# Two plain gate and up pairs become block products: eleven pairs by seven products each

## The chip, the cores and the metric

One core of a Trainium2 chip. The metric is device time in microseconds of one launch; a comparison is made between medians of runs of the kernel before and after. Engines: TensorE (PE, with PEld for its weight loads), VectorE (DVE), ScalarE (ACT), GpSimd (POOL) and SyncE (SP), which issues most loads.

## The reference

A decoder trunk with two layers on 512 positions of width 1024, all in float32. Layer 0 is a gated short convolution, layer 1 an attention layer over a window of 128 with shared keys and values; a SwiGLU feed-forward of width 2816 ends each layer.

```python
def swiglu(h, w_gate_up, w_down):
    g, u = jnp.split(h @ w_gate_up, 2, axis=-1)
    return (jax.nn.silu(g) * u) @ w_down
...
    for l in range(DEPTH):
        if l < N_A:
            mix = short_conv_mixer(rmsnorm(h, a_pre_norm[l]), a_w_in[l], a_conv_w[l], a_w_out[l])
            h = h + rmsnorm(mix, a_post_norm[l])
        else:
            ...
            attn = sliding_window_sink_attention(q, k_sh, v_sh, b_sinks[j]) @ b_w_o[j]
            h = h + rmsnorm(attn, b_post_norm[j])
        ff = swiglu(rmsnorm(h, ffn_pre_norm[l]), ffn_w_gate_up[l], ffn_w_down[l])
        h = h + rmsnorm(ff, ffn_post_norm[l])
```

## The kernel before, in words

Each matmul of the reference is three passes (`mm3`, L189 to L192): every float32 matrix is split into a high part and a low part (`whi`, `wlo` of a weight, `xhi`, `xlo` of an input), and low by high, high by high and high by low are added in PSUM. ACT makes a high part by a copy, DVE the low part by a subtraction. A weight is loaded by SP as a `raw` tile of 128 x 1024.

The gate and up weights come in 22 tiles of 128 columns each, f = 0 to 21, so eleven pairs of tiles. Pairs 0 and 1 (f below `PLAIN` = 4) are multiplied plainly. Pair 0 runs in `project_first`, into four PSUM banks (gate and up of f = 0 and 1), first for the positions 0 to 255 (half 0), then for 256 to 511 (half 1), while the last tile of the residual is still being turned into x. Pair 1 runs in `gate_plain`, 512 positions at a time. The other nine pairs use a scheme of seven products for a two by two block product (Strassen's form): the blocks are the halves of the positions by the halves of the 1024 inputs, and a product is 24 matmuls of 256 columns (two halves e of the gate and up columns, four blocks k, three passes). The order is P1, P2, P6, P5, P7, P3, P4; three accumulations X, Y and Z hold them, each in two banks, one for each e (`gate_jobs`, L850 to L915). P1, P2 and P3 take blocks of x as they are; P6, P5, P7 and P4 take sums of blocks of x, the factors, which `factors` (L356 to L378) makes on DVE with ACT's high parts, in parallel to pair 1. The sums of weight blocks are made by POOL's DMAs, which accumulate in HBM into `hsum` tiles (class `Sums`, L492; P5, P7, P6 and P3 use them); for a pair listed in `ADDED` only two of the four sums are made so, and DVE adds the other two (L445). The table `BEGIN` says at which place of the program a pair's sums are begun: "c" places are in the convolution, "o" in its projection, "a" in the attention, `0f1` or `0p2` in a feed-forward.

`Update` makes x: `take` and `scale` collect the projection, `mean`, `update` and `norm` apply two root mean squares, whose reciprocal root `ur` POOL computes; `turn` transposes four tiles into banks `xt`, `split` makes x hi on ACT (L336) and x lo on DVE (L337), and `keep` copies the parts of the sums (L354). `in_line` walks a list of jobs: each job's weight is fetched `N_RAW` ahead, and split three jobs (`LINE_LEAD`) ahead. Inside the feed-forward the order of instructions of every engine is the order of the program (`manual_schedule`); in the convolution and the projection a scheduler sets it. One launch runs, in time: convolution to about 139 us, its projection to 184, feed-forward 0 to about 510, keys, values and attention to about 690, projection and feed-forward 1 to the end.

Of the kernel before, what the change touches and what calls it, by code (L numbers as in the profile page):

```python
# [24 lines left out]
PLAIN = 4  # L25

ADDED = (0, 1, 2, 6, 7, 8)

BEGIN = {
# [4 lines left out]
}  # L34

ADDED = (0, 1, 2, 6, 7, 8)

BEGIN = {
# [23 lines left out]
NB = 4  # L62
# [12 lines left out]
def yoco_kernel(  # L75
# [10 lines left out]
    w_gu: bass.AP,  # L86
# [143 lines left out]
    class Update:  # L230
# [3 lines left out]
        def __init__(self, mix, gain, gpres, add):  # L234
            self.mix, self.gpres, self.add = mix, gpres, add
            self.gain = gain
# [93 lines left out]
        def split(self, n, f, hf):  # L330
            if self.x[n][f] is None:
                self.x[n][f] = (slot("xhi", F32R), slot("xlo", F32R))
            hi, lo = self.x[n][f]
            c = slice(hf * 256, (hf + 1) * 256)
            src = self.banks[f % 4, hf][:, (f // 4) * 256 : (f // 4 + 1) * 256]
            nc.scalar.activation(hi[:, c], src, AF.Copy, scale=g(self.gpres[n], f))  # L336
            nc.vector.scalar_tensor_tensor(  # L337
                out=lo[:, c], in0=src, scalar=g(self.gpres[n], f), in1=hi[:, c].bitcast(F32),
                op0=ALU.mult, op1=ALU.subtract,
            )  # L340

        def keep(self, b, hf, vector=False):

            for i in range(2):
                if (i, hf, b // 2) not in self.parts:
                    self.parts[i, hf, b // 2] = slot("part")
                out = self.parts[i, hf, b // 2][:, (b % 2) * 256 : (b % 2 + 1) * 256]
                src = self.banks[b, hf][:, i * 256 : (i + 1) * 256]
                gain = g(self.gpres[0], b + 4 * i)
                if vector:  # L350
                    nc.vector.tensor_scalar(out=out, in0=src, scalar1=gain, scalar2=None,
                                            op0=ALU.mult)
                else:
                    nc.scalar.activation(out, src, AF.Copy, scale=gain)  # L354

        def factors(self):  # L356


            x = self.x[0]
            made = {p: [] for p in range(1, 8)}  # L360
            for p, k0, c in ((1, 0, 0), (2, 4, 0), (3, 4, 256)):
                made[p] = [[a[:, c : c + 256] for a in x[k0 + k]] for k in range(4)]
            for j in range(2):
                q11, q21, q12, q22 = (self.parts[i, hf, j] for hf in range(2) for i in range(2))

                nc.vector.tensor_tensor(out=q11, in0=q11, in1=q12, op=ALU.subtract)
                nc.vector.tensor_tensor(out=q12, in0=q22, in1=q12, op=ALU.subtract)
                nc.vector.scalar_tensor_tensor(out=q22, in0=q22, scalar=-1.0, in1=q11,
# [63 lines left out]
    class Job:  # L432
# [14 lines left out]
        def prepare(self):  # L447
            if not self.raws:
                return
# [9 lines left out]
    def in_line(jobs, late):  # L459
# [21 lines left out]
        for j, job in enumerate(jobs):  # L481
# [5 lines left out]
            if late and not job.alone:  # L487
                late.pop(0)()
# [197 lines left out]
    def tile_done(res, t, ahead=None, square=True):  # L686
# [8 lines left out]
        if t > 0:  # L695
            res.norm(t - 1)
# [830 lines left out]
```

## Time and profile before

| | us |
|---|---|
| median of three runs | 1044.12 (1041.91 to 1044.95) |
| span of the profiled execution | 1043.2 |
| TensorE busy in it | 1031.6 (99%) |
| DVE busy | 761.4 (73%) |
| ACT busy | 552.5 (53%) |
| POOL busy | 170.6 (16%) |

The span runs from the first to the last instruction. A busy time counts an instruction from start to end, and matmuls overlap. In a row of the timeline stand start, length, engine, line, operation, what is written from what, and in brackets the idle time before it and what released it.

### The profile page before, as it was taken

Reading aid. Unit: us, or ns where it says so; the run is one execution under the profiler, and the core shown is the slowest. Engines: PE = TensorE matmul, PEld = TensorE weight load, DVE = VectorE, ACT = ScalarE, POOL = GpSimd, SP = SyncE. Lnnn points to the kernel's source line nnn. Section 1 sums busy time; section 2 is a strip of 40 time slices with the busy share of each in tenths; the row PEclk is TensorE's granted clock in tenths of the full one; section 3 lists DMA queues with packets and bytes.
Section 4 is the critical chain, followed back from the end, with each engine's and each line's share of the span. In section 5 each row is a group of like instructions: output and inputs, shape, how many; then the busy total and the mean of one; then the engine's idle time right before and its main releaser. Section 6 shows DMA issues by size and latency. Waiting matters only on the chain.

```text
span 1043.2 us, 17017 instructions
## 1 busy us (share of the span) xinstructions
PE 1031.6 (99%) x6556; PEld 931.4 (89%) x6556; DVE 761.4 (73%) x1280; ACT 552.5 (53%) x994; POOL 170.6 (16%) x227
## 2 busy tenths in 40 slices
PE   9999999999999999999999999999999999999997
PEld 7888888989879899999898888889998999989986
DVE  5675645488676978776658998685886777896754
ACT  7222235746645455464466777666565554645531
POOL 0322231122201000000021554211211110000001
PEclk9999999999999999999999999999999999999999
DMA  9657798568969955337413588967789697534521
GB/s 333 229 176 242 183 321 303 135 184 266 316 232 311 348 175 195 123 120 233 172 42 98 145 250 234 311 215 223 177 283 339 197 322 246 184 125 159 173 89 80
DMA packets 61297, 221.48 MB, mean 212 GB/s; under 512 B 7200, under 2 KB 8096, under 8 KB 51488
## 3 DMA queue, kind: packets, MB, share of 16 engines
q1 hardware_dynamic: 48608, 140.04, 37.2%
q0 software_dynamic: 12032, 79.70, 29.7%
q8 instruction: 51, 0.84, 0.3%
q10 hardware_dynamic: 576, 0.66, 0.2%
q14 instruction: 30, 0.25, 0.1%
HBM read 214.08 MB, written 85.98 MB: 288 GB/s over the span
## 4 chain that ended last, share of the span: by engine, by line
PE 89%; DVE 4%; DMA 3%; issue 1%; ACT 1%; POOLq 0%; POOL 0%; DVEq 0%; SPq 0%; ACTq 0%
PE gx L192 6%; PE gx L191 6%; PE gx L190 6%; PE pmix L191 5%; PE pmix L192 5%; PE pmix L190 5%; PE gz L192 3%; PE gz L191 3%; PE gz L190 3%; PE pgu L190 3%; PE pgu L191 3%; PE pgu L192 3%; PE px L190 2%; PE px L191 2%; PE px L192 2%; PE pcub L594 2%
## 5 line engine op out<-in xcount | busy, mean ns | idle before, releaser
L455 DVE TENSOR_TENSOR wlo<-raw,whi 128x1024 fp32r<-128x1024 f32 (+1 forms) x188 | 227.7, 1214 | 94.4 <-ACT whi L454 94.4
L454 ACT ACTIVATE whi<-raw 128x1024 fp32r<-128x1024 f32 (+1 forms) x188 | 194.6, 1049 | 82.7 <-DVE raw L445 26.6
L190 PE MATMUL gx<-xt,whi 128*128 128x256 f32 x432 | 122.3, 283 | 0.0
L191 PE MATMUL gx<-xt,whi 128*128 128x256 f32 x432 | 122.3, 283 | 0.0
L192 PE MATMUL gx<-xt,wlo 128*128 128x256 f32 x432 | 122.3, 283 | 0.0
L190 PEld LDWEIGHTS gx<-xt,whi 128*128 128x128 f32 x432 | 82.9, 192 | 0.0
L191 PEld LDWEIGHTS gx<-xt,whi 128*128 128x128 f32 x432 | 82.9, 192 | 0.0
L192 PEld LDWEIGHTS gx<-xt,wlo 128*128 128x128 f32 x432 | 82.9, 192 | 0.0
L521 POOL DMA_DIRECT2D hsum<-in_w_gb_dram x84 | 55.9, 717 | 120.5 <-ACT whi L454 81.0
L872 ACT ACTIVATE st<-gx 128x256 f32<-128x256 f32 x72 | 27.5, 381 | 84.2 <-PE gx L192 84.2
L289 POOL TENSOR_TENSOR ur<-uv,mhalf 128x1 f32<-128x1 f32 x15 | 11.6, 774 | 358.3 <-DVE uv L285 358.3
L185 ACT ACTIVATE whi<-raw 128x1024 fp32r<-128x1024 f32 x30 | 31.8, 1058 | 65.3 <-PE pb L191 26.3
L190 PE MATMUL pgu<-xlo,whi 128*128 128x256 f32 (+1 forms) x192 | 61.6, 321 | 0.0
L191 PE MATMUL pgu<-xhi,whi 128*128 128x256 f32 (+1 forms) x192 | 61.1, 318 | 0.0
L192 PE MATMUL pgu<-xhi,wlo 128*128 128x256 f32 (+1 forms) x192 | 61.1, 318 | 0.0
L186 DVE TENSOR_TENSOR wlo<-raw,whi 128x1024 fp32r<-128x1024 f32 x30 | 49.7, 1665 | 2.9 <-ACT whi L185 2.9
L190 PE MATMUL pmix<-wlo,ahi 128*128 128x512 f32 (+1 forms) x136 | 51.3, 377 | 0.0
L191 PE MATMUL pmix<-whi,ahi 128*128 128x512 f32 (+1 forms) x136 | 51.2, 377 | 0.0
L192 PE MATMUL pmix<-whi,alo 128*128 128x512 f32 (+1 forms) x136 | 51.2, 377 | 0.0
L521 POOL DMA_DIRECT2D hsum<-hsum x24 | 19.2, 825 | 153.2 <-ACT whi L454 87.8
L180 DVE TENSOR_TENSOR wlo<-raw,whi 128x512 fp32r<-128x512 f32 x50 | 33.8, 722 | 12.9 <-ACT whi L179 9.6
L190 PE MATMUL gz<-xlo,whi 128*128 128x256 f32 x144 | 40.8, 283 | 0.0
(279 smaller groups left out, 3201.5 us busy)
## 6 DMA issues: line engine op xcount, KB each, us to landing
hsum<-in_w_gb_dram POOLq DMA_DIRECT2D x84, 512.0 KB, 8.8
raw<-hsum SPq DMA_DIRECT2D x72, 512.0 KB, 8.0
raw<-in_w_gb_dram SPq DMA_DIRECT2D x54, 512.0 KB, 5.5
raw<-in_w_dn_dram SPq DMA_DIRECT2D x34, 512.0 KB, 4.8
hsum<-in_w_dn_dram POOLq DMA_DIRECT2D x24, 512.0 KB, 8.0
raw<-in_w_in_dram SPq DMA_DIRECT2D x21, 512.0 KB, 7.0
hsum<-hsum POOLq DMA_DIRECT2D x20, 512.0 KB, 7.4
hsum<-in_w_dn_dram POOLq DMA_DIRECT2D x12, 768.0 KB, 10.8
```

Of the source, the lines that this page charges most:

```text
L180: nc.vector.tensor_tensor(out=lo[:, c], in0=raw[:, c], in1=hi[:, c].bitcast(F32), op=ALU.subtract)
L185: nc.scalar.activation(hi, raw, AF.Copy)
L186: nc.vector.tensor_tensor(out=lo, in0=raw, in1=hi.bitcast(F32), op=ALU.subtract)
L190: nc.tensor.matmul(out, whi, xlo, start=start, stop=False, **kw)
L191: nc.tensor.matmul(out, whi, xhi, start=False, stop=False, **kw)
L192: nc.tensor.matmul(out, wlo, xhi, start=False, stop=stop, **kw)
L289: nc.gpsimd.tensor_tensor(out=self.r[:, t : t + 1], in0=self.v[:, t : t + 1], in1=mhalf[:, :1], op=ALU.pow)
L454: self.begun = nc.scalar.activation(hi[:, :n], raw, AF.Copy)
L455: nc.vector.tensor_tensor(out=lo[:, :n], in0=raw, in1=hi[:, :n].bitcast(F32), op=ALU.subtract)
L521: nc.gpsimd.dma_start(dst, src, max_dma_last_dim=4 * 4 * S, **kw))
L594: nc.tensor.matmul(ps, (whi, whi, wlo)[i][:, kk], (xhi, xlo, xhi)[i], start=k == i == 0, stop=k == KT - 1 and i == 2)
L872: nc.scalar.activation(s, x, AF.Copy)
```

## The change: what it does

All eleven pairs run as block products. The two halves e of a product share one PSUM bank, and one take of 512 columns serves both. Pairs 0 and 1 are the early ones (called a and b): P1 and P2 of both run interleaved with the transposes at the opening, then P3(a) and P3(b), then a list of fifteen products of the pairs 0, 1 and 2 written out by hand. `factors` becomes `add_parts` and `factor(p)`, spread over this list. In half 1 the splits and keeps alternate for each block. `BEGIN` is new: sums start at other places, and pair q of before is pair q + 2; 40 more DMAs are issued by POOL. `ADDED` lists five pairs instead of six.

```diff
-PLAIN = 4
-
-ADDED = (0, 1, 2, 6, 7, 8)
+PAIRS = NF // 2
+
+ADDED = (3, 4, 8, 9, 10)
 
 BEGIN = {
...
-    "c0": "g00", "c2": "g01", "c4": "d00", "c6": "g02", "o0": "g03", "o1": "d01", "0f1": "g04",
...
+    "c0": "g00", "c1": "g01", "c3": "g02", "c5": "g03", "c6": "d00", "o0": "g04", "o1": "g05",
...
+            def products(self, p, w, ks=range(4), pool=None):
+                c = CHAIN[p]
+                opened = c not in self.banks and self.open(c, pool)
+                opened = opened or (self.early and p in (1, 2) and ks[0] == 0)
+                ends = p in (2, 3, 4) or (self.early and p == 5)
+                for e in range(2):
+                    for k in ks:
+                        kk = slice(e * S + k * P, e * S + (k + 1) * P)
+                        mm3(self.banks[c][:, e * 256 : (e + 1) * 256], w[0][:, kk], w[1][:, kk],
+                            *factors[p][k], opened and e == 0 and k == 0,
+                            ends and e == 1 and k == 3, skip_group_check=True)
...
+                if k == 6:
+                    for f in range(4):
+                        before.turn(f, (3,))
+                    for f in range(4):
+                        before.split(0, f + 4, 1)
+                        before.keep(f, 1, 0)
+                        before.keep(f, 1, 1, True)
...
+            def sums(n):
+                for gate in (a, b)[n : n + 1]:
+                    gate.take(2)
+                before.add_parts(n)
...
+            jobs += [early(a, ahead.ready[4], ps_pt, lambda: sums(0)),
+                     early(b, ahead.ready[5], ps_sc, lambda: (sums(1), make(6)()))]
+            made = [gate.jobs(pair_sums, acts[0]) for gate in gates[:3]]
+            opening = [(2, 1), (2, 2), (0, 6), (0, 5), (0, 7), (1, 6), (0, 4), (1, 5), (1, 7),
+                       (2, 6), (1, 4), (2, 5), (2, 7), (2, 3), (2, 4)]
+            jobs += [made[g][p] for g, p in opening]
+            jobs[2].then, jobs[3].then = make(5), make(7)
+            jobs[4].then = lambda: (make(4)(), sum_on(f"{l}f3"))[2:]
```

How it moves instructions is shown at three places. First, ACT at half 1 of layer 0, with x hi of the second four blocks (`xt_1682` and on are the banks, `part` the copies for the sums). Before:

```order
L336 ACTIVATE xhi_1583<-xt_1682,gt 128x256 [waits DVE_49]
L336 ACTIVATE xhi_1591<-xt_1685,gt 128x256 [waits DVE_49]
L336 ACTIVATE xhi_1595<-xt_1700,gt 128x256 [waits DVE_49]
L336 ACTIVATE xhi_1601<-xt_1703,gt 128x256 [waits DVE_49]
L354 ACTIVATE part_1742<-xt_1682,gt 128x256 [waits DVE_49]
L354 ACTIVATE part_1744<-xt_1682,gt 128x256
L354 ACTIVATE part_1742<-xt_1685,gt 128x256 [waits DVE_49]
L354 ACTIVATE part_1744<-xt_1685,gt 128x256
L354 ACTIVATE part_1748<-xt_1700,gt 128x256 [waits DVE_49]
```

After, the same blocks of half 1 (`x` now holds high and low part in one tile, `xt_1724` and on are the banks):

```order
L334 ACTIVATE x_1768<-xt_1724,gt 128x256 [waits PE_49]
L351 ACTIVATE part_1771<-xt_1724,gt 128x256 [waits DVE_49]
L334 ACTIVATE x_1775<-xt_1727,gt 128x256 [waits PE_49]
L351 ACTIVATE part_1771<-xt_1727,gt 128x256 [waits DVE_49]
L334 ACTIVATE x_1780<-xt_1742,gt 128x256 [waits PE_49]
L351 ACTIVATE part_1783<-xt_1742,gt 128x256 [waits DVE_49]
L334 ACTIVATE x_1787<-xt_1745,gt 128x256 [waits PE_49]
L351 ACTIVATE part_1783<-xt_1745,gt 128x256 [waits DVE_49]
```

DVE beside it, also after the change:

```order
L335 SCALAR_TENSOR_TENSOR x_1768<-xt_1724,gt,x_1768 128x256 [waits Activation_49]
L348 TENSOR_SCALAR part_1773<-xt_1724,gt 128x256 [waits Activation_49]
L335 SCALAR_TENSOR_TENSOR x_1775<-xt_1727,gt,x_1775 128x256 [waits Activation_49]
L348 TENSOR_SCALAR part_1773<-xt_1727,gt 128x256 [waits Activation_49]
L335 SCALAR_TENSOR_TENSOR x_1780<-xt_1742,gt,x_1780 128x256 [waits Activation_49]
L348 TENSOR_SCALAR part_1785<-xt_1742,gt 128x256 [waits Activation_49]
L335 SCALAR_TENSOR_TENSOR x_1787<-xt_1745,gt,x_1787 128x256 [waits Activation_49]
L348 TENSOR_SCALAR part_1785<-xt_1745,gt 128x256 [waits Activation_49]
```

Before, ACT made all x hi ahead of the first part, and all parts of half 1 itself. Now x hi and one part take turns for each block, and DVE makes x lo and the other part of the same bank between them, each waiting for the other engine.

Second, DVE at the start of the jobs of layer 0's feed-forward (`wlo` are low parts of weights, `gr` the results of gate and up, `part` the sums of x, `xt` here the low parts of factors). Before:

```order
L455 TENSOR_TENSOR wlo_1904<-raw_1889,whi_1903 128x1024 [waits DMAHW4_49,Activation_49]
L455 TENSOR_TENSOR wlo_1935<-raw_1891,whi_1934 128x1024 [waits DMAHW5_49,Activation_49]
L834 TENSOR_TENSOR a_365_1885<-gr_1878,a_365_1885 128x256 [waits Activation_49]
L366 TENSOR_TENSOR part_1605<-part_1605,part_1742 128x512
L367 TENSOR_TENSOR part_1742<-part_1744,part_1742 128x512 [waits DVE_49]
L368 SCALAR_TENSOR_TENSOR part_1744<-part_1744,part_1605 128x512 [waits DVE_49]
L370 SCALAR_TENSOR_TENSOR part_1607<-part_1744,part_1607 128x512 [waits DVE_49]
L375 TENSOR_TENSOR xt_1948<-part_1744,xt_1948 128x512 [waits DMAHW0_49,Activation_49]
L375 TENSOR_TENSOR xt_1951<-part_1605,xt_1951 128x512 [waits Activation_49]
L375 TENSOR_TENSOR xt_1954<-part_1742,xt_1954 128x512 [waits DMAHW1_49,Activation_49]
L375 TENSOR_TENSOR xt_1957<-part_1607,xt_1957 128x512 [waits Activation_49]
```

After, from the sums of parts of a on:

```order
L362 TENSOR_TENSOR part_1639<-part_1639,part_1771 128x512
L363 TENSOR_TENSOR part_1771<-part_1773,part_1771 128x512 [waits DVE_49]
L364 SCALAR_TENSOR_TENSOR part_1773<-part_1773,part_1639 128x512 [waits DVE_49]
L458 TENSOR_TENSOR wlo_1865<-raw_1816,whi_1864 128x1024 [waits DMAHW5_49,Activation_49]
L873 TENSOR_TENSOR gr_1810<-gy_1615,st_1808 128x2x256 [waits DMAHW0_49,PE_49]
L362 TENSOR_TENSOR part_1642<-part_1642,part_1783 128x512
L363 TENSOR_TENSOR part_1783<-part_1785,part_1783 128x512 [waits DVE_49]
L364 SCALAR_TENSOR_TENSOR part_1785<-part_1785,part_1642 128x512 [waits DVE_49]
L378 TENSOR_TENSOR xt_1900<-part_1773,xt_1900 128x512 [waits Activation_49]
L378 TENSOR_TENSOR xt_1903<-part_1785,xt_1903 128x512 [waits DMAHW1_49,Activation_49]
L458 TENSOR_TENSOR wlo_1908<-raw_1818,whi_1907 128x1024 [waits DMAHW6_49,Activation_49]
L458 TENSOR_TENSOR wlo_1944<-raw_1820,whi_1943 128x1024 [waits DMAHW7_49,Activation_49]
```

The three sums of parts, all four factors and the weights were one block after two gate results; now the sums of a and b, takes and weights alternate, and each factor's low parts stand just ahead of the weights of the products that use it.

Third, POOL ahead of the first `ur` of layer 0's projection. Before:

```order
L521 DMA hsum_140<-in_w_gb_dram 64x2048
L521 DMA hsum_141<-in_w_gb_dram 64x2048
L521 DMA hsum_138<-in_w_gb_dram 64x2048 [waits DMASW4_49]
L521 DMA hsum_139<-in_w_gb_dram 64x2048 [waits DMASW5_49,DMASW1_49]
L521 DMA hsum_160<-in_w_dn_dram 64x2048 [waits DMASW2_49]
L521 DMA hsum_161<-in_w_dn_dram 64x2048 [waits DMASW3_49]
L521 DMA hsum_162<-in_w_dn_dram 64x2048
L521 DMA hsum_163<-in_w_dn_dram 64x2048
L289 TENSOR_TENSOR ur_1188<-uv_1187,mhalf 128x1 [waits DVE_49]
```

After:

```order
L525 DMA hsum_167<-in_w_dn_dram 96x2048 [waits DMASW5_49,DMASW1_49]
L525 DMA hsum_168<-hsum_166 96x2048 [waits DMASW6_49,DMASW2_49,DMASW0_49]
L525 DMA hsum_146<-in_w_gb_dram 64x2048 [waits DMASW3_49]
L525 DMA hsum_147<-in_w_gb_dram 64x2048
L525 DMA hsum_169<-hsum_168 96x2048 [waits DMASW7_49,DMASW2_49]
L525 DMA hsum_146<-in_w_gb_dram 64x2048 [waits DMASW3_49]
L525 DMA hsum_147<-in_w_gb_dram 64x2048 [waits DMASW4_49]
L525 DMA hsum_148<-in_w_gb_dram 64x2048
L525 DMA hsum_149<-in_w_gb_dram 64x2048 [waits DMASW1_49]
L525 DMA hsum_150<-in_w_gb_dram 64x2048
L525 DMA hsum_151<-in_w_gb_dram 64x2048
L281 TENSOR_TENSOR ur_1222<-uv_1221,mhalf 128x1 [waits DVE_49]
```

`bry` of the convolution's last block stood at row 37 before, with 16 DMAs between it and `ur`; it stands at row 48 now, with 19 behind it, of which the down weights' sum `hsum_166` to `hsum_169` was at another place.

More of the change, by code (lines that the diff above doesn't have):

```diff
@@ L340, in split @@
             )
[L342 to L354, printed above, removed]
@@ L486, in in_line @@
                 issue(1 + len(issues) // 6, jobs[j + LINE_LEAD].begun)
-            if late and not job.alone:
-                late.pop(0)()
+            for _ in range(2 if len(late) > 4 else 1):
+                if late and not job.alone:
+                    late.pop(0)()
             late += job.then() or [] if job.then else []
```

309 lines of the change are left out of this document (156 added, 153 removed), and 11 rows, old and new, of the table BEGIN.

## The prediction

> **What bounds the kernel now.** First the page: span, busy times, granted clock, DMA queues.
>
> ```profile
> span 1043.2 us, 17017 instructions
> PE 1031.6 (99%) x6556; PEld 931.4 (89%) x6556; DVE 761.4 (73%) x1280; ACT 552.5 (53%) x994; POOL 170.6 (16%) x227
> PEclk9999999999999999999999999999999999999999
> q1 hardware_dynamic: 48608, 140.04, 37.2%
> q0 software_dynamic: 12032, 79.70, 29.7%
> ```
>
> TensorE works almost without a break at full clock. So the span falls only where TensorE's own work falls, and grows by whatever TensorE comes to wait for. Then the busy times by stretch (columns: TensorE, weight loads, VectorE or DVE, ScalarE or ACT, POOL, clock, DMA share, GB/s); these are the opening of each feed-forward and the rest of layer 0's:
>
> ```profile
> 184.00:230.00 46.00, 46.00 (x304) 42.32 (x303) 31.02 (x55) 28.40 (x56) 8.45 (x13) 1.00 0.55 149
> 230.00:510.00 280.00, 277.73 (x1930) 260.60 (x1929) 211.43 (x303) 150.06 (x223) 21.57 (x32) 0.99 0.73 234
> 735.00:781.00 46.00, 46.00 (x350) 44.44 (x349) 38.71 (x60) 27.96 (x44) 8.77 (x14) 1.00 0.85 236
> ```
>
> The two openings, which the change rewrites, have no idle TensorE at all, and DVE is 31.02 and 38.71 us busy of 46. TensorE's timeline, third, gives the price of a matmul by the distance of starts (the duration is longer, since matmuls overlap) and the one long wait of the layer:
>
> ```profile
> 208.75 0.28 PE L190 MATMUL pgu<-xlo,whi 128*128 128x256 f32 x1
> 208.87 0.28 PE L191 MATMUL pgu<-xhi,whi 128*128 128x256 f32 x1
> 208.99 0.28 PE L192 MATMUL pgu<-xhi,wlo 128*128 128x256 f32 x1
> 209.11 0.40 PE L190 MATMUL pgu<-xlo,whi 128*128 128x512 f32 x1
> ...
> 230.22 0.39 PE L190 MATMUL pgu<-xlo,whi 128*128 128x512 f32 x1
> 230.45 0.39 PE L191 MATMUL pgu<-xhi,whi 128*128 128x512 f32 x1
> 230.68 0.39 PE L192 MATMUL pgu<-xhi,wlo 128*128 128x512 f32 x1
> 230.90 0.28 PE L190 MATMUL gx<-xlo,whi 128*128 128x256 f32 x1
> ...
> 295.50 0.39 PE L192 MATMUL py<-whi,alo 128*128 128x512 f32 x1
> 298.15 0.50 PE L190 MATMUL px<-wlo,ahi 128*128 128x512 f32 x1 [2.27 <-DVE mix L1002]
> 299.72 0.63 PE L190 MATMUL px<-wlo,ahi 128*128 128x512 f32 x1
> 300.15 0.63 PE L191 MATMUL px<-whi,ahi 128*128 128x512 f32 x1
> ```
>
> A product 256 columns wide costs 0.120 us and one of 512 costs 0.227 us ((230.90 - 209.11) / 96). The wait at 295.50 costs 2.65 - 0.23 = 2.4 us, and some eight matmuls at 0.43 instead of 0.23 us follow: 1.6 us more.
>
> **TensorE's saving.** Per layer the two plain pairs are 2 x 2 x 8 x 2 x 3 products of 256 for the first pair and 2 x 2 x 8 x 3 of 512 for the second: 192 x 0.120 + 96 x 0.227 = 44.8 us. As block products they are 2 x 7 x 24 = 336 of 256: 40.3 us. That is -4.5 us per layer, -9.0 us in all, and certain as long as TensorE stays fed.
>
> **What fed it, and no longer does.** The 96 products of 512 (209.11 to 230.90) need no sums of blocks. Under them DVE makes the factors of the sums:
>
> ```profile
> 213.15 0.68 DVE L366 TENSOR_TENSOR part<-part,part 128x512 f32<-128x512 f32 x1
> 213.87 0.69 DVE L367 TENSOR_TENSOR part<-part,part 128x512 f32<-128x512 f32 x1
> ...
> 221.35 2.50 DVE L375 TENSOR_TENSOR xt<-part,xt 128x512 fp32r<-128x512 f32 x4
> 223.87 1.23 DVE L455 TENSOR_TENSOR wlo<-raw,whi 128x1024 fp32r<-128x1024 f32 x1
> ```
>
> That is 10.7 us, 213.15 to 223.87, hidden because first use is at 230.90. After the change the first factor is wanted five products of 24 behind the opening's first half: P3(a), P3(b), then pair 2's P1 and P2, then P6(a).
>
> *First wait, P3(a).* It is the first user of the second half's columns. Today these are split in two rows of instructions, first all x, then all parts (the three rows behind the dots group the same instructions, with the mean of one in ns ahead of the second bar):
>
> ```profile
> 195.71 3.02 ACT L336 ACTIVATE xhi<-xt,gt 128x256 fp32r<-128x256 f32 x8 [2.12 <-PE xt L327]
> 198.58 3.08 ACT L354 ACTIVATE part<-xt,gt 128x256 f32<-128x256 f32 x8
> 196.22 3.23 DVE L337 SCALAR_TENSOR_TENSOR xlo<-xt,gt,xhi 128x256 fp32r<-128x256 f32 x8 [4.44 <-ACT xhi L336]
> ...
> L337 DVE SCALAR_TENSOR_TENSOR xlo<-xt,gt,xhi 128x256 fp32r<-128x256 f32 x8 | 3.2, 474 | 4.4 <-ACT xhi L336 4.4
> L354 ACT ACTIVATE part<-xt,gt 128x256 f32<-128x256 f32 x8 | 3.1, 554 | 0.0
> L336 ACT ACTIVATE xhi<-xt,gt 128x256 fp32r<-128x256 f32 x8 | 3.0, 489 | 2.1 <-PE xt L327 2.1
> ```
>
> Eight x lo come 0.40 us apart from 196.22. In the new order each block is ACT x hi, DVE x lo, ACT part, DVE part on one bank, and each waits for the one ahead; a round on ACT is 0.49 + 0.47 + about 0.40 (a part's spacing) plus handoffs of some 0.04, 1.47 us. The four x lo that P3 needs, if the first is ready at 196.7, are ready at 196.7, 198.2, 199.7, 201.1. P3(a) stands 96 products of 256 before 209.11, so at 197.6; its fourth block starts at 201.1 and five blocks of three products remain (1.8 us): it ends at 202.9 instead of 200.5. Stall 2.4 to 2.7 us. The Trainium skill, "PSUM — Partial Sum Buffer", section "PSUM bank collisions raise a hardware error", says that two engines may not touch one bank's same partitions in one cycle, reads against reads included, and that the compiler's scheduler adds a dependency for it; by that rule the rounds are serial as above, and without it they would be 0.8 us (two DVE instructions) and the sum 2.5 us per layer less. No row here shows two engines reading one bank at once.
>
> *The following waits.* With DVE never idle from here I add its new rows up in their order: a weight low part of 1024 1.15 us (two in 2.36 in the row below), anything of 512 0.65 to 0.72 us, ACT 1.0 for 1024 and 0.55 for 512.
>
> ```profile
> 210.54 2.36 DVE L455 TENSOR_TENSOR wlo<-raw,whi 128x1024 fp32r<-128x1024 f32 x2 [0.26 <-ACT whi L454]
> 209.45 2.00 ACT L454 ACTIVATE whi<-raw 128x1024 fp32r<-128x1024 f32 x2
> ```
>
> DVE starts the first weight low part at 203.65 (ACT has two copies of sums and the weight's high part ahead of it), then the take, three part sums, a weight, a take, three part sums: 211.5. The two lows of factor 6 follow at 212.1 and 212.75; the weight of P6(a) waits on ACT (factor, copy of P3(b), weight: 213.6) and is done at 214.85. TensorE is through P3(b), P1(2), P2(2) at 202.9 + 3 x 2.88 = 211.6: it waits 3.0 us. The take of P6(a) stands behind another weight and factor 7's lows: P7(a) waits 0.8 us; P4(a) waits for the take of P7 behind factor 4: 2.0 us. Sum with P3: 8.5 us per layer by this ladder. The lower bound lets every handoff vanish and keeps DVE's work up to that take: 8 x 0.40 (x lo and parts) + 7 x 1.15 (weights) + 6 x 0.65 (takes) + 8 x 0.72 (part sums) + 8 x 0.65 (factor lows) = 26.1 us from 196.2 on, so 222.3, where TensorE unhindered comes to P4(a) eight products behind 197.6, at 220.6: 1.7 us. Since the waits stand in the order row by row I lean to the ladder, but its handoffs are estimates; I take 7 per layer, 14 for both. Layer 1 opens with the same instructions, and its old opening leaves DVE less room (38.71 us busy). The Trainium skill, "TensorE: Matmul & The Clock Gate", section "Part 1: The HAM clock gate", has TensorE fall to half rate after an idle window of some 3.4 us; the row at 299.72 agrees as far as a 2.4 us wait was followed by slow matmuls. By that a long wait would add about 1.6 us, which would lift the sum by up to 3.
>
> **POOL's queue.** POOL issues the DMAs that sum weights and, behind them, the small `ur` that the update of the residual waits for.
>
> ```profile
> hsum<-in_w_gb_dram POOLq DMA_DIRECT2D x84, 512.0 KB, 8.8
> 139.00:184.00 45.00, 45.00 (x209) 37.49 (x208) 22.76 (x34) 21.64 (x41) 6.29 (x11) 1.00 0.89 305
> ...
> 152.92 2.30 POOL L521 DMA_DIRECT2D hsum<-in_w_dn_dram  x4
> 168.14 0.57 POOL L289 TENSOR_TENSOR ur<-uv,mhalf 128x1 f32<-128x1 f32 x1 [12.92 <-DVE uv L285]
> 179.53 1.16 ACT L316 ACTIVATE xn<-h,ur 128x1024 f32<-128x1024 f32 x1 [1.44 <-POOL ur L311]
> 181.23 1.91 PE L327 MATMUL xt<-ident,xn 128*128 128x128 f32 x16
> 132.25 0.85 POOL L521 DMA_DIRECT2D hsum<-hsum  x1 [5.41 <-DMA hsum<-hsum]
> ```
>
> POOL has 12.9 us to spare now. After the change a larger group (shown in the order of POOL's rows above) stands behind the last two gates of the convolution, which come at about 125 as at present; it holds 22 DMAs with about six waits for landings of 5 to 9 us (5.41 of waiting in the last row, a median of 8.8 from issue to landing in the first). I get 160 to 175 for its end. Up to 168 costs nothing, 175 costs 7 less the spare 1.2: 5.5 us. I take 2.
>
> **DMA.** 144 transfers of POOL take 0.297 x 1043.2 = 310 us of the 16 engines, 2.15 each; 40 more are 86 us. SP's 16 more at about 1.4 (140 MB in 388 us, half a MB each) are 23. Share 67% becomes 77%; in 230 to 510 it was 0.73, with 0.27 x 280 = 75 us free for about 30 to 40 of it. The sums are begun several products ahead of their use, so that a later landing of one is not felt at once. I cost it at nothing; bounds: the wait at 295.50 (4.0 us with its slow matmuls) goes, or a like one comes in each layer (+8).
>
> **Sharing of banks.** One bank for both halves: the take of 512 columns (0.65 us) must fit, with at most one weight of 1.15 ahead of it, into the 2.88 us of the next product. It fits with 1 us over, so 0; and it saves instructions off the path.
>
> **Sum.** 1043.2 - 9.0 + 14 + 2 = 1050.2 in the profiled execution; the median of the runs, 1044.12, is 0.9 above its span, so 1051. What a measurement can tell from no change is 0.3%, 3.1 us: 1041.0 to 1047.3.
>
> **Rivals.** *DVE keeps up* (faster side): the waits of the opening come down to DVE's work, 1.7 us per layer, and POOL is in time: 1043.2 - 9.0 + 3.4 + 0.9 = 1038.5. For it: DVE is idle for a third of the old opening, and takes are merged. Against it: the rounds over one bank. It decides where waits fall under 4.5 us per layer. Chance 0.22. *POOL late* on top of the ladder: 1043.2 - 9 + 17 + 5.5 + 0.9 = 1057.6; for it the tight group of issues, and the DMA share of 0.89 in that stretch, which makes landings long; against it POOL's 12.9 us to spare; 0.14. *The wait at 295.50 goes*: 1051 - 4 = 1047; the sums that collide there are moved, but more data is too; 0.12. *Weights late in the middle* from the fuller DMA: 1051 + 8 = 1059; for it the wait at 295.50, which is of this kind, against it the 27% of DMA time free there; 0.08. *The sharing itself stalls* at each take: 0.3 us a product would be 154 x 0.3 = 46 us; excluded nearly by the 1 us over; 0.01.
>
> **How the numbers follow.** The forecast itself, 1051 (1047 to 1056 by itself), has 0.43. Faster than 1041.0: most of the first rival and a little of the third, 0.23. Within: the rest of these and the forecast's low edge, 0.17. Slower: 0.60. The range runs from DVE keeping up to late weights: 1039 to 1059.
>
> **What would show it.** Right: P3(a)'s products wait for DVE x lo four times near 198 to 201; P6(a) waits for its weight, P7(a) and P4(a) for takes on DVE; the same in layer 1; `ur` after 168 and the transposes after 181.23. Wrong: no wait over 1 us between 197 and 231, DVE idle there; or new waits outside the opening, with ACT's weight parts released by DMA.

## The result, and the profile after

The changed kernel takes 1080.74 us (median of 4 runs, 1079.52 to 1082.0) against 1044.01 before: ratio 1.036, interval 1.0343 to 1.0378. It is slower by 36.7 us, where 7 were forecast and the range ended at 1059. The page of the changed kernel:

```profile
span 1077.8 us, 17185 instructions
PE 1032.5 (96%) x6652; PEld 934.5 (87%) x6652; DVE 771.8 (72%) x1214; ACT 553.5 (51%) x926; POOL 199.1 (18%) x267
q1 hardware_dynamic: 50912, 148.43, 37.9%
q0 software_dynamic: 15232, 100.68, 36.0%
```

TensorE was idle 11.6 us of the span before and 45.3 us now. The view of waits for TensorE (us in total, times, longest) names the new ones:

```profile
PE xt L319 <- ACT xn L308: 10.6, 3, 5.5
PE pz L181 <- DVE wlo L458: 8.9, 2, 7.4
PE gx L181 <- DVE st L873: 3.4, 2, 1.7
PE gz L181 <- DVE x L335: 3.1, 4, 0.8
PE px L181 <- DVE wlo L458: 2.7, 2, 1.6
PE px L181 <- DVE mix L983: 1.7, 1, 1.7
PE gx L183 <- DVE wlo L458: 1.5, 2, 0.8
```

A wait also costs the slow matmuls behind it. So I summed, by stretch, the distance between the starts of successive matmuls beyond the usual one (0.120 us for 256 columns, 0.227 for 512, 0.109 for a transpose):

| place (us in the changed kernel) | before | after | difference |
|---|---|---|---|
| up to the end of the convolution | 4.6 | 3.6 | -1.0 |
| layer 0's update, transposes (150 to 205) | 0.0 | 12.7 | +12.7 |
| layer 0's opening (205 to 245) | 0.0 | 7.9 | +7.9 |
| layer 0's middle (245 to 345) | 4.2 | 13.9 | +9.7 |
| attention (525 to 715) | 3.3 | 4.7 | +1.3 |
| layer 1's opening with the transposes (715 to 775) | 0.1 | 8.7 | +8.7 |
| layer 1's first down products (775 to 900) | 0.0 | 3.2 | +3.2 |

These sum to +42.5. The saving is as forecast: 192 starts of 512 columns fewer and 288 of 256 more are -43.6 + 34.6 = -9.0. What follows the last matmul is 1.2 longer. Together +34.7, and the spans differ by 34.6.

The timeline of TensorE, after, at the update, the opening and the middle of layer 0:

```profile
184.86 0.33 PE L319 MATMUL xt<-ident,xn 128*128 128x128 f32 x1 [4.51 <-ACT xn L308]
190.66 0.69 PE L319 MATMUL xt<-ident,xn 128*128 128x128 f32 x2 [5.47 <-ACT xn L308]
...
211.24 0.39 PE L181 MATMUL gz<-x,whi 128*128 128x256 f32 x1 [0.78 <-DVE x L335]
212.66 0.58 PE L181 MATMUL gz<-x,whi 128*128 128x256 f32 x1 [0.79 <-DVE x L335]
226.14 0.39 PE L183 MATMUL gx<-xt,wlo 128*128 128x256 f32 x1 [0.76 <-DVE wlo L458]
232.41 0.36 PE L181 MATMUL gx<-xt,whi 128*128 128x256 f32 x1 [0.50 <-DVE gr L873]
240.09 0.35 PE L181 MATMUL gx<-xt,whi 128*128 128x256 f32 x1 [1.70 <-DVE st L873]
...
296.60 0.76 PE L181 MATMUL pz<-wlo,ahi 128*128 128x512 f32 x1 [7.41 <-DVE wlo L458]
```

The opening waits where the prediction put its waits: P3(a) at 211 and 212.7 for x lo, P6(a) at 226.1 for its weight, P7(a) and P4(a) for takes on DVE. Behind P3(a)'s waits the granted clock is 0.50 for 3.41 us, from 212.50 on and, in layer 1, from 741.57 on; the slow matmuls there are 1.5 us of each opening's sum. Of layer 1's 8.7 us, 0.8 is a wait of the transposes at 721. The two large groups are elsewhere. The first is POOL's queue ahead of `ur` (timeline of POOL, after; the last row is POOL's longest wait for a landing in this stretch before):

```profile
146.88 0.82 POOL L525 DMA_DIRECT2D hsum<-in_w_dn_dram  x1 [11.06 <-DMA hsum<-in_w_dn_dram]
150.79 0.82 POOL L525 DMA_DIRECT2D hsum<-in_w_dn_dram  x1 [3.09 <-DMA hsum<-in_w_dn_dram]
161.22 0.80 POOL L525 DMA_DIRECT2D hsum<-hsum  x1 [9.62 <-DMA hsum<-in_w_dn_dram]
...
171.62 0.83 POOL L525 DMA_DIRECT2D hsum<-hsum  x1 [8.55 <-DMA hsum<-hsum]
...
178.08 0.85 POOL L281 TENSOR_TENSOR ur<-uv,mhalf 128x1 f32<-128x1 f32 x1
...
149.48 0.81 POOL L521 DMA_DIRECT2D hsum<-in_w_gb_dram  x1 [10.62 <-DMA hsum<-in_w_gb_dram]
```

The steps of the sum d00 wait for the landings of those ahead of them, 11.1, 3.1, 9.6 and 8.6 us one after another, and `ur` comes at 178.08, 9.9 us later than the 168.14 of before; its input `uv` was ready on DVE at 167.02. The second is the fetch of raw weights. Queues and issues between 240 and 300 us, after, then before, then ACT's wait that holds TensorE until 296.6 (columns of an issue: count, KB each, median us to landing):

```profile
q0 software_dynamic: 1781, 11.71, 71.4%
raw<-hsum SPq DMA_DIRECT2D x5, 512.0 KB, 21.0
raw<-in_w_dn_dram SPq DMA_DIRECT2D x3, 512.0 KB, 25.2
...
q0 software_dynamic: 1372, 8.92, 51.2%
raw<-hsum SPq DMA_DIRECT2D x6, 512.0 KB, 14.1
raw<-in_w_dn_dram SPq DMA_DIRECT2D x3, 512.0 KB, 12.8
...
294.14 1.06 ACT L457 ACTIVATE whi<-raw 128x1024 fp32r<-128x1024 f32 x1 [8.78 <-DMA raw<-hsum]
```

POOL's sums take 71.4% of the 16 engines there instead of 51.2%, a weight needs 21 to 25 us instead of 13 to 14, and the prefetch, which is some jobs deep, no longer covers that.

### The profile page after: what moved, and what is told of

Its sections match the earlier page's. It is cut to its first block, busy times and chain, and to the rows that moved or that the text cites. A ratio compares the mean times of both kernels' runs of the same rounds, so it can differ in the third digit from the quotient of the medians.

```text
span 1077.8 us, 17185 instructions
## 1 busy us (share of the span) xinstructions
PE 1032.5 (96%) x6652; PEld 934.5 (87%) x6652; DVE 771.8 (72%) x1214; ACT 553.5 (51%) x926; POOL 199.1 (18%) x267
## 4 chain that ended last, share of the span: by engine, by line
PE 69%; DMA 13%; DVE 9%; ACT 4%; issue 3%; POOL 1%; POOLq 0%; SPq 0%; DVEq 0%; ACTq 0%
DMA raw<-hsum 7%; PE gx L181 6%; PE gx L183 6%; PE gx L182 6%; PE gz L181 3%; PE gz L182 3%; PE gz L183 3%; PE pmix L181 3%; PE pmix L182 3%; PE pmix L183 3%; DMA hsum<-in_w_dn_dram 3%; PE px L181 2%; PE px L182 2%; PE px L183 2%; DMA hsum<-in_w_gb_dram 2%
## 5 line engine op out<-in xcount | busy, mean ns | idle before, releaser
L181 PE MATMUL gx<-xt,whi 128*128 128x256 f32 x528 | 149.9, 284 | 4.5 <-DVE st L873 3.4
L183 PE MATMUL gx<-xt,wlo 128*128 128x256 f32 x528 | 149.6, 283 | 1.5 <-DVE wlo L458 1.5
L182 PE MATMUL gx<-xt,whi 128*128 128x256 f32 x528 | 149.4, 283 | 0.0
L525 POOL DMA_DIRECT2D hsum<-in_w_gb_dram x112 | 73.6, 737 | 178.3 <-ACT whi L457 116.2
L181 PEld LDWEIGHTS gx<-xt,whi 128*128 128x128 f32 x528 | 101.3, 192 | 5.6 <-issue 5.1
L183 PEld LDWEIGHTS gx<-xt,wlo 128*128 128x128 f32 x528 | 101.3, 192 | 1.9 <-DVE wlo L458 1.9
L182 PEld LDWEIGHTS gx<-xt,whi 128*128 128x128 f32 x528 | 101.3, 192 | 0.0
L876 ACT ACTIVATE st<-gx 128x512 f32<-128x512 f32 x40 | 23.6, 596 | 77.9 <-PE gx L183 74.6
L181 PE MATMUL gz<-x,whi 128*128 128x256 f32 x176 | 51.7, 294 | 3.4 <-DVE x L335 3.1
L182 PE MATMUL pmix<-whi,ahi 128*128 128x512 f32 (+1 forms) x136 | 51.2, 377 | 0.0
L183 PE MATMUL pmix<-whi,alo 128*128 128x512 f32 (+1 forms) x136 | 51.2, 377 | 0.0
L182 PE MATMUL gz<-x,whi 128*128 128x256 f32 x176 | 51.2, 291 | 0.0
L183 PE MATMUL gz<-x,wlo 128*128 128x256 f32 x176 | 51.1, 290 | 0.0
L281 POOL TENSOR_TENSOR ur<-uv,mhalf 128x1 f32<-128x1 f32 x15 | 11.6, 776 | 212.7 <-DVE uv L277 212.7
L181 PE MATMUL gy<-x,whi 128*128 128x256 f32 x176 | 50.3, 286 | 0.0
L181 PE MATMUL gz<-xt,whi 128*128 128x256 f32 x176 | 49.8, 283 | 0.0
```

The lines of the kernel that those rows point to most:

```text
L181: nc.tensor.matmul(out, whi, xlo, start=start, stop=False, **kw)
L182: nc.tensor.matmul(out, whi, xhi, start=False, stop=False, **kw)
L183: nc.tensor.matmul(out, wlo, xhi, start=False, stop=stop, **kw)
L281: nc.gpsimd.tensor_tensor(out=self.r[:, t : t + 1], in0=self.v[:, t : t + 1], in1=mhalf[:, :1], op=ALU.pow)
L525: nc.gpsimd.dma_start(dst, src, max_dma_last_dim=4 * 4 * S, **kw))
L876: nc.scalar.activation(s, self.banks["X"], AF.Copy)
```

## The experiments

Theory: three causes, each with its own repair: `ur` behind POOL's queue, fetches behind a full set of DMA engines, and DVE's order in the opening. Rival: one cause, full DMA engines, or a DVE that simply has too much to do. A ratio is to the kernel before, run beside the experiment.

### One edit each, and all three

**e1_ur_dve.** In `mean` and `mean2`:

```diff
-            nc.gpsimd.tensor_tensor(out=self.r[:, t : t + 1], in0=self.v[:, t : t + 1],
-                                    in1=mhalf[:, :1], op=ALU.pow)
+            nc.vector.tensor_scalar(out=self.r[:, t : t + 1], in0=self.v[:, t : t + 1],
+                                    scalar1=-0.5, scalar2=1.5, op0=ALU.mult, op1=ALU.add)
...
-            nc.gpsimd.tensor_tensor(out=self.r[:, i : i + 1], in0=self.v[:, i : i + 1],
-                                    in1=mhalf[:, :1], op=ALU.pow)
+            nc.vector.tensor_scalar(out=self.r[:, i : i + 1], in0=self.v[:, i : i + 1],
+                                    scalar1=-0.5, scalar2=1.5, op0=ALU.mult, op1=ALU.add)
```

The kernel leaves out the root in both layers; a straight line stands in its place.

> The power that makes ur (means of the residual's updates) is replaced by one DVE instruction, a line -0.5 v + 1.5, so it no longer stands behind POOL's DMA issues; every DMA stays. Theory 'POOL's queue': the two waits of TensorE for the transposes at 180 and 185 us (4.7 and 5.7 us, and about 2 us of slow matmuls behind them) go, 1080.7 falls by 11 to 13 us to about 1068. Rival 'the DMA engines are the limit': the update waits for something else that is late, for instance the weights of the opening, and the time falls by less than 4 us, or TensorE waits later by as much at 288 us.

Measured: 1064.83 us, span 1061.8, 16.0 below the changed kernel's, where 11 to 13 were expected. The excess at the update is gone (12.7 to 0.0); the middle keeps 12.4 of 13.9. The rest of the gain is 0.8 at layer 1's down products and 0.9 ahead of layer 1's opening, whose `ur` is a line too. POOL's queue is shown as the cause of the first group.

**e3_apart.** In the opening's half 1:

```diff
                     for f in range(4):
                         before.split(0, f + 4, 1)
+                    for f in range(4):
                         before.keep(f, 1, 0)
                         before.keep(f, 1, 1, True)
```

> Only the order of half 1 is changed in both layers: first the four splits of x, then the eight parts. Theory 'turns on one bank': P3(a) is fed 0.8 us per block at most, its 2.5 us of wait per layer goes, 5 us in all: about 1075.5. Rival 'DVE's work is the bound': the parts come later by as much, P6(a) waits longer by what P3(a) waits less, and the time stays within 1.5 us of 1080.7.

Measured: 1074.53 us, span 1070.8, down 7.0: opening 7.9 to 5.1 in layer 0 and 8.7 to 6.0 in layer 1, the rest in the middle (13.9 to 11.3), which this edit was not meant to touch. P3(a) still waits once per layer, now for a part:

```profile
PE gz L181 <- DVE part L348: 1.3, 2, 0.7
PE gx L181 <- DVE st L873: 3.4, 2, 1.7
```

The order of half 1 is worth 2.7 to 2.8 us per layer, what the prediction gave for the turns on one bank, though in other parts: P3(a)'s waits fall from 2.3 and 2.4 us to 0.9, the 1.5 us of slow matmuls behind them go, and P6(a) waits some 0.3 longer. P4(a)'s wait for a take (second row) did not grow in exchange.

**e4_added.**

```diff
-ADDED = (3, 4, 8, 9, 10)
+ADDED = (3, 4, 5, 6, 7, 8, 9, 10)
```

> Pairs 5, 6 and 7 get two sums by DMA instead of four (DVE adds the other two): 12 transfers of sums and 6 fetches fewer per layer, as many pairs with four sums as before. Theory 'the DMA engines are full': raw weights land in 10 to 20 us instead of 20 to 33 us between 257 and 300 us, the waits at 288, 317 and 322 us and those at 814 and 818 us shrink, together by 8 to 14 us: about 1070. Rival 'order on the queue': SP issues its fetches too late whatever the load, the time falls by under 3 us. The wait of ur behind POOL's queue is not touched in either.

Measured: 1061.24 us, span 1059.5, down 18.3, where 8 to 14 were expected. All excess in the middle (13.9) and at layer 1's first down products (3.2) is gone, also the 4.2 that the kernel before has there. Issues and queue of 240 to 300 us in this run:

```profile
q0 software_dynamic: 1440, 9.44, 60.8%
raw<-hsum SPq DMA_DIRECT2D x8, 512.0 KB, 12.6
raw<-in_w_dn_dram SPq DMA_DIRECT2D x3, 512.0 KB, 13.3
```

POOL's share falls to 60.8% and a weight lands in 13 us, as before. DVE's six adds of 1.2 us per layer cost nothing that shows.

**e2_all3**, the three together:

> The three edits together (ur as a line on DVE, the order of half 1, two sums for the pairs 5, 6 and 7). If the three causes are apart their gains add up: 12 + 5 + 10 = 27 us, about 1054. If they are one cause, full DMA engines, the sum is hardly more than that of the largest single edit.

Measured: 1042.45 us, ratio 1.0004 (0.9992 to 1.0016). The spans fall by 16.0, 7.0 and 18.3 singly, 41.3 in sum, and by 36.0 together: three causes. The 5.3 us between are about what is counted twice in the sum: e1 and e3, by shifting the work, relieve the middle and layer 1's down products by 2.4 and 3.2 us, and e4 takes all of both. What is left is 5.1 us of waits in each opening.

### The load of the DMA engines without the change

**e7_before_more**, the kernel before with only this edit:

```diff
-ADDED = (0, 1, 2, 6, 7, 8)
+ADDED = (6, 7, 8)
```

> The kernel before, with ADDED = (6, 7, 8): the pairs 2 to 4 of the block products get four sums by DMA, as in the change, so 12 more transfers of sums and 6 more fetches per layer; opening, BEGIN and banks are the old ones. Theory 'full DMA engines': raw weights land later and TensorE comes to wait between 270 and 330 us and near 800 us, +8 to +16 us, about 1055. Rival 'it takes the new BEGIN or the new opening': under +3 us.

Measured: 1062.79 us, ratio 1.0203 (1.0182 to 1.0223), 21.3 us above the kernel before beside it, where 8 to 16 were expected, and for the most part not by the expected way. More sums alone do bring TensorE's waits into the kernel before, with its own opening. But the place of the kernel before's wait at 295.50 (third row) has 5.1 us of excess and had 4.2. The rest is `ur` behind POOL's queue in both layers: 7.9 us of excess at layer 0's update and 10.2 more than before at layer 1's, where DVE stood idle for 9.3 us until `ur` had come (at 700.17; TensorE's 4.1 us for `mixo` hang on that update). So this run is evidence for POOL's queue, and the evidence for late fetches is e4. Nor is its load quite the change's: besides the pairs 5 to 7 of both kernels, here 2, 3 and 4 get four sums, in the change 0, 1 and 2.

```profile
PE xt L327 <- ACT xn L316: 7.2, 3, 5.0
PE pmix L190 <- DVE mixo L253: 4.1, 1, 4.1
PE px L190 <- DVE mix L1002: 3.2, 1, 3.2
```

### Moving transfers instead of leaving them out

**e5_d00_late.** In BEGIN:

```diff
-    "c0": "g00", "c1": "g01", "c3": "g02", "c5": "g03", "c6": "d00", "o0": "g04", "o1": "g05",
-    "0f1": "d01", "0f3": "g06", "0p1": "g07", "0p2": "d02", "0p3": "g08", "0s0": "g09",
+    "c0": "g00", "c1": "g01", "c3": "g02", "c5": "g03", "o0": "g04", "o1": "g05",
+    "0f0": "d00", "0f1": "d01", "0f3": "g06", "0p1": "g07", "0p2": "d02", "0p3": "g08", "0s0": "g09",
```

> One entry of BEGIN moved: the sums of round 0's down weights (d00) begin at 0f0, behind the update, not at c6 ahead of it; the number of transfers is the same and ur stays on POOL. Theory 'POOL's queue': ur is in time (168 us or earlier), the 12 us at 180 to 195 go, about 1069, unless the moved transfers make raw weights later. Rival 'full DMA engines': the same load later makes the waits at 288 to 325 us longer by about what is won, the time stays above 1076.

Measured: 1077.52 us, span 1075.9: the rival's number. `ur` is in time (first row), and the waits come back in the middle (25.6 us of excess in place of 13.9), for weights that land late: between 240 and 300 us they take 26.5 and 29.4 us (medians of the sums and of the down weights), and the wait at 265.15 hangs on DVE's sum of two weights (second row).

```profile
166.90 0.57 POOL L281 TENSOR_TENSOR ur<-uv,mhalf 128x1 f32<-128x1 f32 x1 [15.79 <-DVE uv L277]
...
261.70 1.23 DVE L447 TENSOR_TENSOR raw<-raw,raw 128x1024 f32<-128x1024 f32 x1 [3.85 <-DMA raw<-hsum]
...
265.15 0.58 PE L181 MATMUL gx<-xt,whi 128*128 128x256 f32 x1 [4.22 <-ACT st L876]
...
291.00 0.77 PE L181 MATMUL pz<-wlo,ahi 128*128 128x512 f32 x1 [5.48 <-DVE wlo L458]
```

So transfers ahead of the update hold up `ur`, and the same transfers behind it hold up the fetches. The two causes are separate mechanisms that share one budget.

### The opening

**e8_pair2_only.** Pair 2 made early, its P3 ahead of P6(a):

```diff
-        gates = [Gates(q, q < 2) for q in range(PAIRS)]
+        gates = [Gates(q, q < 3) for q in range(PAIRS)]
...
-            opening = [(2, 1), (2, 2), (0, 6), (0, 5), (0, 7), (1, 6), (0, 4), (1, 5), (1, 7),
-                       (2, 6), (1, 4), (2, 5), (2, 7), (2, 3), (2, 4)]
+            opening = [(2, 1), (2, 2), (2, 3), (0, 6), (0, 5), (0, 7), (1, 6), (0, 4), (1, 5),
+                       (1, 7), (2, 6), (1, 4), (2, 5), (2, 7), (2, 4)]
```

> Pair 2 is made early too (its P3 by itself), and P3 of pair 2 goes ahead of P6(a): one more product of 2.9 us that needs no factor stands between P3(b) and the first factor. Theory 'DVE is behind by its work': the waits ahead of P6(a), P7(a) and P4(a), 1.3 + 0.7 + 1.9 us per layer, fall to under 1 us per layer, 6 us in all: about 1075. Rival 'each wait is a handoff of its own': the waits stay, moved by one product, and the time stays within 1.5 us of 1080.7.

Measured: 1080.77 us, no change, and the experiment tells less than it was meant to: factor 4 hangs on `jobs[4]`, which was P6(a) and is P3 of pair 2 now, so it came ahead of the take of P6(a). P7(a), which needs that take, waits 2.7 us (TensorE's row; the profile names ACT's copy, which ended last, but in the program's order the matmul waits for the take, the last of DVE's rows):

```profile
238.16 0.55 PE L181 MATMUL gx<-xt,whi 128*128 128x256 f32 x1 [2.73 <-ACT st L882]
...
234.73 0.69 DVE L378 TENSOR_TENSOR xt<-part,xt 128x512 fp32r<-128x512 f32 x1 [0.70 <-ACT xt L377]
...
236.72 0.69 DVE L378 TENSOR_TENSOR xt<-part,xt 128x512 fp32r<-128x512 f32 x1 [0.70 <-ACT xt L377]
237.33 0.68 DVE L873 TENSOR_TENSOR gr<-gx,gr 128x512 f32<-128x512 f32 x1
```

What it does show is factor 4's form: twice DVE stands still for 0.70 us while ACT makes a high part, with takes queued behind.

**e9_hand**, on e2_all3:

```diff
-            for gate in (a, b):
-                gate.take(1)
...
+                    if gate is a:
+                        for g1 in (a, b):
+                            g1.take(1)
                     gate.products(3, w, pool=pool)
...
                 if p == 4:
                     nc.vector.scalar_tensor_tensor(out=q21, in0=q22, scalar=-1.0, in1=q21,
                                                    op0=ALU.mult, op1=ALU.subtract)
+            for j in range(2):
+                q11, q21, q12, q22 = (self.parts[i, hf, j] for hf in range(2) for i in range(2))
```

> On the kernel with the three edits (ur as a line on DVE, half 1 with splits first, two sums for pairs 5 to 7): ACT makes the first weight's high part ahead of the copies of P1(a) and P1(b), and factor 4 makes both its sums first and then the high and low parts. DVE's work stays the same, its idle time in the opening (1.2 us ahead of the first weight, 0.7 twice in factor 4) goes. Theory 'handoffs between ACT and DVE': the waits ahead of P6(a), P7(a) and P4(a), 3.4 us per layer, fall by 2 to 3 us, 1042.5 becomes about 1037. Rival 'DVE has too much work there': within 1 us of 1042.5.

Measured: 1038.82 us, ratio 0.9953 (0.9941 to 0.9965), 3.6 below e2_all3; P6(a)'s wait for its weight (first row) falls from 0.8 to 0.4 us, P4(a)'s (second row) from 1.7 to 0.3:

```profile
PE gx L183 <- DVE wlo L460: 0.8, 2, 0.4
PE gx L181 <- DVE st L875: 0.6, 2, 0.3
```

**e11_fewer_lows**, on e2_all3: the subtractions for factors 5 and 7 are left out.

```diff
-                nc.vector.tensor_tensor(out=lo, in0=q, in1=hi.bitcast(F32), op=ALU.subtract)
+                if p in (5, 7):
+                    lo = self.lows[j]
+                else:
+                    nc.vector.tensor_tensor(out=lo, in0=q, in1=hi.bitcast(F32), op=ALU.subtract)
+                if p == 6:
+                    self.lows = getattr(self, "lows", []) + [lo]
```

> On the kernel with the three edits: factors 5 and 7 use the low parts of factor 6, so that DVE leaves out four subtractions of 512 columns per layer, 2.6 us; nothing else moves. Theory 'DVE has too much work there': the waits ahead of P7(a) and P4(a) fall by up to 2.5 us per layer, 1042.5 becomes 1037 to 1039. Rival 'handoffs between ACT and DVE': DVE comes to wait for ACT instead, under 1.5 us in all.

Measured: 1039.21 us, ratio 0.9967 (0.9948 to 0.9986), 0.2 above the upper end of what the work theory gave. Taking 2.6 us of DVE's work per layer and taking its idle time win much the same, 3.2 and 3.6 us of the medians, or 3.8 and 4.7 of TensorE's excess in the two openings: these two runs don't tell work from handoffs, since the take stands behind both in DVE's one queue.

### Nothing left out

**e6_pair2** joins the order of half 1, the longer ADDED, the moved d00 of e5 and the early pair 2 of e8.

> All repairs on the changed kernel with nothing left out: half 1 with splits first, two sums for the pairs 5 to 7, d00 begun at 0f0, pair 2 early. If the four causes are apart: waits left in the opening about 2 us per layer, none in the middle, TensorE's 9 us saved: 1044 - 9 + 4 = 1039, between 1035 and 1042. If d00 now collides with the fetches: 1044 or more.

Measured: 1057.41 us, ratio 1.0155 (1.0138 to 1.0172). The 1039 is missed, and the second case came about: d00 behind the update brings waits at 254 and at 266 to 267 us even with fewer sums (3.7 and 2.3 us of excess), and pair 2 brings e8's 2.7 us twice.

**e10_d00_early** keeps ADDED, half 1 and the handoffs, and begins d00 at c2:

```diff
-    "c0": "g00", "c1": "g01", "c3": "g02", "c5": "g03", "c6": "d00", "o0": "g04", "o1": "g05",
+    "c0": "g00", "c1": "g01", "c2": "d00", "c4": "g02", "c6": "g03", "o0": "g04", "o1": "g05",
```

> Nothing left out: the changed kernel with half 1 split first, two sums for pairs 5 to 7, the handoffs of the opening as in e9_hand, and the sums of d00 begun at c2 (g02 at c4, g03 at c6) so that POOL's queue is shorter ahead of ur while ur stays on POOL. If the causes are as told: ur in time or under 2 us late, about 1039, between 1035 and 1043. If the convolution's own fetches starve by the earlier sums: waits before 139 us and 1045 or more.

Measured: 1044.77 us, ratio 1.0023 (1.0012 to 1.0035). The update loses nothing more (`ur` comes 0.9 us behind its `uv`), but the convolution's last gates come late. DVE's last `bry` starts at 149.15 (first row), in the changed kernel at 138.96, and TensorE waits at the projection for it; the wait and the slow matmuls there are some 5 us. What put the gates late in the scheduler's order is not shown.

```profile
149.15 0.69 DVE L652 TENSOR_TENSOR bry<-cut,bry 128x512 f32<-128x512 f32 x1
...
150.55 0.54 PE L181 MATMUL pmix<-wlo,yhi 128*128 128x512 f32 x1 [2.86 <-ACT yhi L654]
```

**e12_g04_late** keeps the convolution's entries and moves g04 and g05 behind the update:

```diff
-    "c0": "g00", "c1": "g01", "c3": "g02", "c5": "g03", "c6": "d00", "o0": "g04", "o1": "g05",
-    "0f1": "d01", "0f3": "g06", "0p1": "g07", "0p2": "d02", "0p3": "g08", "0s0": "g09",
+    "c0": "g00", "c1": "g01", "c3": "g02", "c5": "g03", "c6": "d00", "0f0": "g04",
+    "0f1": "d01", "0f3": "g05", "0p0": "g06", "0p1": "g07", "0p2": "d02", "0p3": "g08", "0s0": "g09",
```

> Nothing left out, convolution's entries of BEGIN as in the change: half 1 split first, two sums for pairs 5 to 7, the opening's handoffs as in e9_hand, ur on POOL, and the sums g04 and g05 begun behind the update (0f0, 0f3; g06 at 0p0) in place of o0 and o1, so that only the sums d00 stand in POOL's queue ahead of ur. If POOL's queue and the load are the whole matter: ur at 168 to 170 us, no wait at 147 us as in e10, none over 2 us from 240 to 330 us, about 1039 (1037 to 1042), below the kernel before. If the eight transfers moved behind the update fill the engines again: waits between 240 and 330 us and 1044 or more.

Measured: 1047.58 us, ratio 1.0038 (1.0023 to 1.0054). `ur` comes at 168.42, and eight transfers more behind the update are enough to fill the engines there: between 240 and 300 us POOL's share is 59.5%, in e9 it is 45.8%, and a weight takes 17.6 to 23.0 us, in e9 10.9 to 14.4.

```profile
168.42 0.57 POOL L281 TENSOR_TENSOR ur<-uv,mhalf 128x1 f32<-128x1 f32 x1 [4.18 <-DVE uv L277]
...
PE px L181 <- ACT mix L983: 5.7, 2, 3.8
```

**e13_sqrt** moves no transfer, but takes the root off POOL in layer 0, in a function that `mean` and `mean2` call:

```diff
+        def root(self, i):
+            r, v = self.r[:, i : i + 1], self.v[:, i : i + 1]
+            if not self.add:
+                nc.scalar.activation(v, v, AF.Sqrt)
+                nc.vector.reciprocal(r, v)
+            else:
+                nc.gpsimd.tensor_tensor(out=r, in0=v, in1=mhalf[:, :1], op=ALU.pow)
...
```

> As e9_hand, but with the computation whole: in layer 0's update ACT takes a square root and DVE its reciprocal in place of POOL's power; layer 1 keeps POOL. The sums' transfers stay where the change put them. If POOL's queue was the whole of the wait at 180 to 195 us: 1039 to 1041, below the kernel before by 0.2 to 0.5%, with one table load of 1.3 us on ACT more. If the gain of the runs with a line came from work left out: the transposes come late again and it is 1045 or more.

Measured: 1040.48 us (11 runs), ratio 0.9988 (0.9979 to 0.9998): the one version with nothing left out that is faster than the kernel before. The time is as expected, the gain, about a tenth of a percent, is under the 0.2 that were expected, and under the 0.3% that the prediction took as what a measurement can tell. The 12.7 us at the update become 2.0. ACT's table load ahead of the first root takes 1.28 us, but most of it passes before `uv` is ready at 168.08, and it ends at 168.53, so it can hold up the root by 0.5 us at most; where the rest of the 2.0 us comes from no run takes apart.

```profile
167.25 1.28 ACT L279 ACT_TABLE_LOAD   x1
167.87 0.21 DVE L285 TENSOR_SCALAR uv<-us 128x1 f32<-128x1 f32 x1
...
PE xt L325 <- ACT xn L314: 2.2, 2, 1.6
```

## Why the prediction was wrong, step by step

- **TensorE's saving, -9.0**: right, by the count of starts.
- **The opening, 14 (7 per layer)**: right in place and nearly in size, 7.9 in each layer, besides the 0.8 of layer 1's transposes. The ladder's 8.5 was nearer than the 7 taken. Its steps: x lo came 1.42 us apart (207.86 to 212.13) where 1.47 was reckoned, and P3(a)'s waits cost 2.3 and 2.4 as said; P7(a) 0.7 and P4(a) 1.9, as said. P6(a) cost 1.3 to 1.4 and not 3 (3.25 by the ladder's own 214.85 and 211.6; and four products stand ahead of it behind the first half, not five). The 1.5 us of matmuls at half clock behind P3(a) are why: DVE caught up by as much meanwhile. In e4 the clock stayed full in layer 0's opening, P6(a) cost 2.8 there, and the opening's sum was 7.9 all the same. So the half rate, for which the prediction allowed up to 3, cost nothing by itself in the opening.
- **POOL's queue, 2 with bounds 0 and 5.5**: this step failed. The estimate of 160 to 175 for the end of the group rested on landings of 5 to 9 us, the median of all sums. The d00 sums are 768 KB each and ran with the engines full (a share of 1.01 to 1.04 by stretches of 10 us from 130 to 180); POOL waited 11.1, 3.1, 9.6 and 8.6 us for them one after another. The end was 178, `ur` 9.9 late. The profile before had it: a DMA share of 0.89 in that stretch, and POOL's timeline a wait of 10.6 us there, at 149.48. And the slow transposes and matmuls behind the wait, about 2.3 us, were not in the sum.
- **DMA, 0 with bounds -4 and +8**: this step failed too: +9.7 in layer 0 and +3.2 in layer 1. I reckoned free time over 230 to 510 as a whole, 75 us; the added sums fall into 240 to 300, where the engines were full already (before, by stretches of 10 us, a share of 1.01, 0.70, 1.00, 1.02, 1.05 and 1.02). An average over a stretch hid the place. The row that spoke for it was the wait at 295.50 itself, and I let it count as a chance of 0.08.
- **Sharing of banks, 0**: right as far as shown: with the load repaired (e4, e2, e9) the excess from 245 to 525 is nil.
- **The rivals**: "POOL late" and "weights late in the middle" both came true, at once, and on top of the opening. I gave each by itself, with the others at their middle, and the range ended at the largest single one. They share a cause, more transfers, so they were likely together: with 10.7 more at the update and 12.9 of late weights 1051 becomes 1074.6. The opening adds 2.6, the attention and the end 1.3 and 1.2, the convolution takes 1.0, and the median lies 2.9 above its profiled span and not 0.9: 1080.7.

## What to carry to other kernels

Price added DMA work at the place where it lands: look at the share of the engines by stretches of 10 us or so, and where it is at 1 already, expect landings there to take longer (here 21 to 25 us for 13 to 14), and every in-order queue that waits for landings with them. Ask of each small instruction on the path which queue it stands in, and behind which waits; with the other repairs in, moving the instruction (e13, 1040.48) was better than moving the transfers (e10, 1044.77, and e12, 1047.58). When several rivals have one cause, add them.

## What the runs showed of the hardware that I had not expected

A fetch of 512 KB took 5 to 8 us as a median of the whole run before, and 21 to 25 us between 240 and 300 us of the changed kernel, with POOL's sums at 71% of the engines; 11 points off that share (e4) brought it to 13. The share alone does not set it: in e12, at 59.5%, the same fetches took 17.6 and 23.0 us, in e4, at 60.8%, 12.6 and 13.3. What else does is not shown.

The clock: in these traces it is granted at 1.00 or 0.50, and its changes lie at whole multiples of 3.41 us from each other (in the changed kernel at 185.19, 195.44, 212.50, 215.91, 294.42, 301.25, 741.57 and 744.98). Behind TensorE's wait of 7.4 us at 288.8, matmuls of 512 started 0.43 us apart for 4.4 us, while waits of 1.6 to 1.9 us (240.09, 319.72, 324.45) were followed by no slow ones. Yet P3(a)'s two waits of 0.8 us were (first two rows, the clock is the third number from the end), and the same waits in layer 0 of e4 were not (last row):

```profile
209.09:212.50 3.41, 1.87 (x12) 1.28 (x10) 2.32 (x6) 1.81 (x5) 0.00 (x0) 1.00 0.93 263
212.51:215.90 3.39, 3.24 (x15) 3.25 (x16) 1.41 (x3) 2.39 (x4) 0.00 (x0) 0.50 0.02 8
...
212.50:216.00 3.50, 3.21 (x26) 3.21 (x27) 1.52 (x3) 3.23 (x6) 0.00 (x0) 1.00 0.01 4
```

What sorts them is the sum of what TensorE lost (starts farther apart than usual) within one of these windows of 3.41 us. In the 15 traces, every window at full clock that lost 2.06 us or more was followed by one at half clock, 32 of them, and none that lost 1.99 or less. P3(a)'s waits and the lesser delays beside them lost 2.20 in one window (from 209.09 on); in e4 a border between windows parted them into 1.36 and 1.09. The kernel before lost 2.12 (296.15 to 299.56) and went to half rate; P4(a)'s wait in layer 1, 1.94, cost nothing more. The Trainium skill, "TensorE: Matmul & The Clock Gate", section "What's actually happening", gives an idle window of some 3.4 us, free-running. The length and the free run agree with the traces; but no window had to be idle throughout, 2.06 us of it were enough. So the slow matmuls at 299.72, which the prediction read as agreement, agree with the length alone.
